# Values' projection as seven block products of halves, in one piece under the scores of head 0

## The chip, the cores and the metric

The kernel runs on one core of one Trainium2 chip. The metric is the device time of one execution in microseconds; before the change the median of three runs is 856.49 us (856.48 to 856.85). TensorE is called PE here, VectorE DVE, ScalarE ACT, GpSimd POOL, and SyncE, which issues most DMAs, SP. Each engine works through its own queue in order.

## What is computed

One block of a streaming encoder on 512 tokens of 1024 features, in float32. Cut to what matters here:

```python
xn = rmsnorm(x, norm_mix_g)
q, k, v, xr, gr, ga, gb = split(xn @ w_in)           # seven parts of 1024 columns each
ya = chunked_band_attention(q, k, v, rel_table) @ w_attn_out   # 16 heads of 64
yb = (rg_lru(conv(xr)) * gelu(gr)) @ w_rnn_out
h = x + (sigmoid(ga) * ya + sigmoid(gb) * yb) @ w_o
gu = rmsnorm(h) @ w_ffn_in
out = rmsnorm(h + (silu(g) * up) @ w_ffn_out)
```

The values `v = xn @ W_v` are a product of 512x1024 by 1024x1024. `W_v` is a slice of `w_in`.

## The kernel before

Every float32 operand is held as two parts, a high one (`hi`, a copy on ACT, line L82) and the remainder (`lo`, a subtraction on DVE, line L83); the helper `split` issues both. One product of two such operands is three matmuls, in the helper `mm3` (lines L76, L77, L78). `whl_...` is a weight tile in both parts, `raw_...` the same tile as it came from memory.

PE works through these stages: norms and transposes of x (until 38 us); the gated branch (`xr`, `gr`, `gb`, convolution and scan), until 166 us, with the first pair of heads' queries and keys `q0`, `k0` at its end; values' tiles of group 0; scores of head 0; `yb`, the product with `w_rnn_out` (189 to 233 us); the sixteen heads with the rest of `q`, `k`, `v` and gate `ga` between them (233 to 432 us); `ya`; the product with `w_o`; the FFN.

Values: `v_tile(gr, t)` computes 128 tokens by 512 columns, 24 matmuls with tokens stationary. There are two groups of columns of four tiles each; group 0 stands ahead of `yb`, group 1 between the heads.

Heads: PE's order is written by hand. In the loop over heads each head h is: transposes of its probabilities (`transposed`, tiles `pT`, split into `pp`), scores of head h+1 (`scores`, tiles `s`), the tiles named in `laid[h]` left of the bar, the product with the values (`weigh`, tile `o`, added up in `oacc`), the tiles right of the bar. After the scores DVE adds the bias and reduces (L740), ACT takes the exponential (L741), DVE the reciprocal of the sums `rl` (L742) and POOL scales the four blocks of probabilities `p` (L744), which the next transposes read.

`k_tile` leaves `kh` and `kl` of two heads: for each, ACT copies the own half of the partitions (L686), DVE subtracts (L687), ACT copies into the other half (L688) and POOL casts (L689). Scores of the pair's first head read both halves.

Products with `w_o` and the FFN matrices are already made as seven products of halves instead of eight. For these the sums of weight blocks are made early, by `spill` and `spill_in`: SP loads four blocks (tiles `spill...`), DVE forms the four sums one on the other, SP stores them to memory (`sums...`), and the stage that uses them loads them again. Here `w_o`'s are made in the gated branch, those of `w_ffn_out`'s first unit and of the FFN-in tiles `fg2`, `fu2` during `yb`.

Of the kernel before, what the change touches and what calls it, by code (L numbers as in the profile page):

```python
# [36 lines left out]
def block_kernel(ctx: ExitStack, tc: tile.TileContext, x, norm_mix_g, w_in, b_merge, rel_table,  # L37
# [478 lines left out]
    def rnn_gates(j, xc, xch, g):  # L516
# [22 lines left out]
        dve.scalar_tensor_tensor(ti[:], ti[:], 1.0, xc[:], ALU.add, ALU.mult)  # L539
        return j, u, a, ti, g  # L540

    def rnn_scan(j, u, a, ti, g):
        dve.scalar_tensor_tensor(ti[:], ti[:], 0.5, u, ALU.mult, ALU.mult)
        dve.tensor_tensor_scan(u, a[:], ti[:], 0.0, ALU.mult, ALU.add)
        dve.scalar_tensor_tensor(u, u, 0.5, g[:], ALU.mult, ALU.mult)
        if j % 2 == 0:
# [2 lines left out]
        act.activation(o[:, 0], u, AF.Copy)
        pool.tensor_sub(o[:, 1], u, f(o[:, 0]))  # L550
        return o
# [47 lines left out]
    def spill(w, unit, to, r):  # L599
# [4 lines left out]
        for out_, i, a_, b_ in ((b11, 0, b12, b11), (b12, 2, b22, b12), (b22, 1, b22, b11), (b21, 3, b21, b22)):  # L604
# [4 lines left out]
            if out_ is b22:  # L609
                sp.dma_start(out=to[0][:], in_=b11)  # L610

    def spill_of(w, u, pl, tag, bufs):
        name, unit, to = (("o", units_o, sums_o) if w is w_o else ("f", units, sums_d))
# [89 lines left out]
    for k in (4, 6):
        homes["v0", k] = (aw, "v", 8, 1)

    def v_tile(gr, t):
        wv = weights(f"v{gr}")
        po = mm_tile(f"po_v{gr}_{t}", "mm" if gr else "t")
        for k in range(KT):
            mm3(po[:], xnT[k][:, 0, t * P:(t + 1) * P], xnT[k][:, 1, t * P:(t + 1) * P],  # L710
                wv(0, k, every), wv(1, k, every), k == 0, k == KT - 1)
        v = aw.tile([P, 4, 4, HD], F32R, tag="v", bufs=8, name=f"v{gr}_{t}")
        split(v[:, :, 0::3], v[:, :, 1:3], po[:].rearrange("p (a b d) -> p a b d", a=4, b=2))
        vs.setdefault(gr, []).append(v)
# [49 lines left out]
    def weigh(h, pp):  # L764
        pr, e = divmod(h, 2)
        own, other = halves(e)
        if e == 0:
            oacc.append(tg_.tile([P, S], F32, tag="tg", name=f"oacc{pr}"))
        acc = oacc[pr]
        po = mm_tile(f"o{h}")  # L770
        for kb in range(NT):
            i, lo, n = ((0, 0, 512), (1, 0, 384), (2, 0, 256), (2, 256, 128))[kb]
            st = vs[pr // 4][kb][:, pr % 4, 2 * e:2 * e + 2].rearrange("p a d -> p (a d)")
            for part in range(2):
                pe.matmul(po[:, S - n:S], st, pp[i][:, part, lo:lo + n], start=kb == 0 and part == 0, stop=kb == NT - 1 and part == 1)  # L775
        act.activation(acc[own, :], po[other, :], AF.Copy)
# [21 lines left out]
    kinds = {"q": q_tile, "k": k_tile, "v": lambda t: v_tile(1, t), "g": gate_a}  # L798

    def project_all(names):  # L800
        for n in names.split():
# [590 lines left out]
```

## Time and profile before

| What | Value |
|---|---|
| Median of the runs | 856.49 us (856.48 to 856.85) |
| Profiled execution | span 854.7 us on the page; no device time of its own is listed |
| PE busy | 845.1 us (99%) |
| DVE, ACT, POOL busy | 642.1, 507.5, 107.5 us |
| Chain that ended last | PE 97% |
| DMA | 135.70 MB, mean 159 GB/s |

The span runs from the first instruction to the last. The chain follows back from the last instruction to what released each step; a share of 97% on PE says that nearly all of the span is PE going from one of its instructions to the next. In rows of groups, the two numbers after the bar are busy microseconds and mean nanoseconds of one instruction; behind the second bar is the idle time ahead of them on that engine. In a timeline row the first two numbers are start and duration in microseconds.

### The profile page before, as it was taken

To read this page: it belongs to the slowest core of one execution; us is meant where nothing else is said; L and a number is where in the kernel's file an instruction comes from. 1 tells how busy PE (TensorE), PEld (TensorE's weight loads), DVE (VectorE), ACT (ScalarE), POOL (GpSimd) and SP (SyncE) were. 2 spreads that over 40 slices of the span, in tenths; PEclk is the share of its full clock that TensorE was granted. 3 is DMA by queue.
4 is the path that set the end of the run, shared out by engine and by line. 5 is a ranking of instruction groups with operands and counts; after the bars stand their busy time and mean duration, and the time that the engine had idled before them with its cause. 6 is when DMAs were issued, how large, how long until landed. Compare 5 with 4: busy or idle time off the path is not lost.

```text
span 854.7 us, 13069 instructions
## 1 busy us (share of the span) xinstructions
PE 845.1 (99%) x4884; PEld 741.0 (87%) x4884; DVE 642.1 (75%) x972; ACT 507.5 (59%) x877; POOL 107.5 (13%) x152
## 2 busy tenths in 40 slices
PE   8999999999999999999999999999999999999997
PEld 6977887888888888888888889999999999988885
DVE  5789767635665657557668877988999887699985
ACT  7678687741366657666654546556555555385555
POOL 2324302200113313223200000000000001000002
PEclk9999999999999999999999999999999999999999
DMA  8594332429852113323156541665666343886622
GB/s 275 190 313 164 99 99 67 120 79 362 274 157 75 59 52 101 98 75 111 50 175 244 157 164 50 201 234 166 241 203 215 100 123 99 275 297 205 209 74 98
DMA packets 103663, 135.70 MB, mean 159 GB/s; under 512 B 6832, under 2 KB 77088, under 8 KB 103600
## 3 DMA queue, kind: packets, MB, share of 16 engines
q1 hardware_dynamic: 99920, 127.20, 45.4%
q10 hardware_dynamic: 3680, 7.67, 2.9%
q8 instruction: 38, 0.62, 0.3%
q14 instruction: 25, 0.20, 0.1%
HBM read 115.93 MB, written 18.92 MB: 158 GB/s over the span
## 4 chain that ended last, share of the span: by engine, by line
PE 97%; ACT 1%; DVE 1%; DMA 1%; issue 0%; POOL 0%; SPq 0%; ACTq 0%; DVEq 0%
PE po_out L76 4%; PE po_out L77 4%; PE po_out L78 4%; PE o L775 2%; PE p_fu L78 2%; PE p_fg L78 2%; PE p_fu L76 2%; PE p_fg L77 2%; PE p_fg L76 2%; PE p_fu L77 2%; PE pT L755 2%; PE po_gb L76 2%; PE po_gb L77 2%; PE po_ga L76 2%; PE po_v L76 2%; PE po_ga L78 2%
## 5 line engine op out<-in xcount | busy, mean ns | idle before, releaser
L744 POOL TENSOR_SCALAR p<-p,rl 128x128 f32<-128x128 f32 (+1 forms) x64 | 39.6, 637 | 164.6 <-DVE rl L742 164.5
L741 ACT ACTIVATE p<-p,m 128x128 f32<-128x128 f32 (+1 forms) x64 | 35.8, 562 | 13.8 <-DVE m L740 13.8
L1104 POOL TENSOR_TENSOR act_lo<-act,act_hi 128x1024 fp32r<-128x1024 f32 x1 | 2.4, 2414 | 294.3 <-ACT act_hi L1103 294.3
L83 DVE TENSOR_TENSOR pp<-pT,pp 128x384 fp32r<-128x384 f32 (+1 forms) x48 | 27.8, 596 | 9.8 <-ACT pp L82 9.7
L740 DVE CUSTOM_DVE_ANT_0 p<-s,bias 128x128 f32<-128x128 f32 (+1 forms) x64 | 29.2, 483 | 3.9 <-PE s L737 3.8
L83 DVE TENSOR_TENSOR whl_t<-raw_t,whl_t 128x1024 fp32r<-128x1024 f32 x26 | 31.9, 1226 | 0.3 <-ACT whl_t L82 0.3
L83 DVE TENSOR_TENSOR whl_qk<-raw_qk,whl_qk 128x1024 fp32r<-128x1024 f32 x16 | 21.6, 1348 | 11.3 <-ACT whl_qk L82 11.3
L76 PE MATMUL po_gr<-xnT,whl_gr 128*128 128x512 f32 (+1 forms) x80 | 28.2, 354 | 0.1
L82 ACT ACTIVATE whl_t<-raw_t 128x1024 fp32r<-128x1024 f32 x26 | 27.2, 1047 | 1.5 <-PE po_h L78 1.5
L77 PE MATMUL po_xr<-xnT,whl_xr 128*128 128x512 f32 (+1 forms) x80 | 27.8, 353 | 0.0
L77 PE MATMUL po_gr<-xnT,whl_gr 128*128 128x512 f32 (+1 forms) x80 | 27.6, 346 | 0.0
L78 PE MATMUL po_gr<-xnT,whl_gr 128*128 128x512 f32 (+1 forms) x80 | 27.6, 348 | 0.0
L78 PE MATMUL po_xr<-xnT,whl_xr 128*128 128x512 f32 (+1 forms) x80 | 27.3, 346 | 0.0
L76 PE MATMUL po_xr<-xnT,whl_xr 128*128 128x512 f32 (+1 forms) x80 | 26.7, 353 | 0.6 <-ACT xnT L362 0.6
L83 DVE TENSOR_TENSOR whl_fg_s<-s_fg,whl_fg_s 128x1024 fp32r<-128x1024 f32 x20 | 24.4, 1222 | 2.9 <-ACT whl_fg_s L82 2.9
L83 DVE TENSOR_TENSOR whl_fu_s<-s_fu,whl_fu_s 128x1024 fp32r<-128x1024 f32 x20 | 24.3, 1221 | 2.9 <-ACT whl_fu_s L82 2.8
L82 ACT ACTIVATE whl_qk<-raw_qk 128x1024 fp32r<-128x1024 f32 x16 | 16.8, 1052 | 16.0 <-PE po_yb L78 8.8
L76 PE MATMUL po_gb<-xnT,whl_gb 128*128 128x512 f32 x64 | 25.3, 395 | 0.2 <-DVE xc L501 0.2
L82 ACT ACTIVATE whl_fu_s<-s_fu 128x1024 fp32r<-128x1024 f32 x20 | 21.0, 1056 | 7.3 <-PE q_fu L78 2.6
L76 PE MATMUL po_ga<-xnT,whl_ga 128*128 128x512 f32 x64 | 25.3, 395 | 0.0
L77 PE MATMUL po_gb<-xnT,whl_gb 128*128 128x512 f32 x64 | 25.1, 393 | 0.0
L82 ACT ACTIVATE whl_fg_s<-s_fg 128x1024 fp32r<-128x1024 f32 x20 | 21.1, 1056 | 6.8 <-DVE s_fg L195 3.9
(421 smaller groups left out, 3261.8 us busy)
## 6 DMA issues: line engine op xcount, KB each, us to landing
raw_fg<-in_w_ffn_in_dram SPq DMA_DIRECT2D x22, 512.0 KB, 3.7
raw_fu<-in_w_ffn_in_dram SPq DMA_DIRECT2D x22, 512.0 KB, 5.0
raw_t<-sums SPq DMA_DIRECT2D x20, 512.0 KB, 4.5
raw_qk<-in_w_in_dram SPq DMA_DIRECT2D x32, 256.0 KB, 3.2
spillf<-in_w_ffn_out_dram SPq DMA_DIRECT2D x16, 512.0 KB, 8.0
sums<-spillf SPq DMA_DIRECT2D x16, 512.0 KB, 4.6
raw_b<-in_w_ffn_out_dram SPq DMA_DIRECT2D x15, 512.0 KB, 4.3
raw_xr<-in_w_in_dram SPq DMA_DIRECT2D x8, 512.0 KB, 4.9
```

What stands on the lines that cost most here:

```text
L76: pe.matmul(o, sh, mh, start=start, stop=False, skip_group_check=parts)
L77: pe.matmul(o, sh, ml, start=False, stop=False, skip_group_check=parts)
L78: pe.matmul(o, sl, mh, start=False, stop=stop, skip_group_check=parts)
L82: act.activation(hi, src, AF.Copy)
L83: dve.tensor_sub(lo, src, f(hi))
L740: dve.tensor_tensor_reduce(prob[qb][:], scs[qb], bias[:, S - w:S], -1.0, 3e38, ALU.add, ALU.min, nmax[:, qb:qb + 1])
L741: act.activation(prob[qb][:], prob[qb][:], AF.Exp, bias=nmax[:, qb:qb + 1], scale=-1.0, accum_out=lsum[:, qb:qb + 1])
L744: pool.tensor_scalar(prob[qb][:], prob[qb][:], rl[:, qb:qb + 1], 1.0, ALU.mult, ALU.mult)
L755: pe.transpose(pt[:, at * P:(at + 1) * P], prob[qb][:, kb * P:(kb + 1) * P], ident[:])
L775: pe.matmul(po[:, S - n:S], st, pp[i][:, part, lo:lo + n], start=kb == 0 and part == 0, stop=kb == NT - 1 and part == 1)
L1104: pool.tensor_sub(lo[:], o[:], f(hi[:]))
```

## The change

Values are computed as seven products of blocks. Features and weights are cut in halves both ways: tokens 0 to 255 and 256 to 511, inner dimension in halves, columns in halves. With blocks `a11` to `a22` of xn and `b11` to `b22` of `W_v`, sums `s1` to `s4` of the first and `t1` to `t4` of the second, the products are `a11 b11`, `a12 b21`, `s1 t1`, `s2 t2`, `s4 b22`, `s3 t3`, `a22 t4`. Each has 256 tokens (two tiles of 128) by 512 columns by 512 inner, that is 2 x 12 matmuls of 128x512. Sums that chain through several products stay in PSUM; others are copied out by ACT (`v_keep`) and added by DVE (`v_finish`).

The whole projection stands between `yb` and the heads, with scores of head 0 between the two token tiles of `s3 t3`. The sums of `W_v` are made in the gated branch, in the place of those of `w_o`; `w_o`'s are made around the start of `yb`; those of `w_ffn_out`'s first unit, `fg2` and `fu2` are called for in heads 1, 4 and 6. The sums of xn are made during `yb`. Group 1's tiles go from `laid`.

```diff
-    laid = ("q1 k1 | v0", "q2 |", "k2 | v1", "q3 |", "k3 | v2", "q4 v3 |", "k4 | q5", "k5 | g0",
-            "g1 |", "q6 | g2", "k6 | g3", "q7 |", "k7 | g4", "g5 |", "g6 |", "g7 |")
+    laid = ("q1 k1 |", "q2 |", "k2 |", "q3 |", "k3 |", "q4 |", "k4 |", "q5 | g0",
+            "k5 | g1", "q6 |", "k6 | g2", "q7 | g3", "k7 | g4", "g5 |", "g6 |", "g7 |")
...
-    for t in range(NT):
-        v_tile(0, t)
...
     for j in range(0, KT, 2):
         if j >= 4:
-            at_once(spill_of(w_o, j // 2 - 2, early, "spill", 4))
+            at_once(spill_of(w_v, j // 2 - 2, early, "spill", 4))
...
+    def wv_part(name, u):
+        n = sources[name]
+        raw = wp.tile([P, 2, S], F32, tag="raw", bufs=3, name=f"raw_v{name}_{u}")
+        sp.dma_start(out=raw[:], in_=sums_v[u][n][:] if name[0] == "t" else square(w_v, units_v[u][n[0]], n[1]))
+        hl = wp.tile([P, 2, 2, S], F32R, tag="whl", bufs=4, name=f"whl_v{name}_{u}")
+        split_pair(hl, raw[:])
+        wv[name, u] = hl
...
+    def v_multiply(a, b, banks, start, tokens=range(2)):
+        for i in tokens:
+            tok = slice(i * P, (i + 1) * P)
+            for u in range(2):
+                w = wv[b, u]
+                for k in range(2):
+                    mm3(banks[i][:], xv_at(a, u, k, 0, tok), xv_at(a, u, k, 1, tok), w[:, 0, k], w[:, 1, k],
+                        start and u == 0 and k == 0, u == 1 and k == 1, parts=True)
...
+    def v_split(gr, t, src):
+        v = v_of(gr, t)
+        split(v[:, :, 0::3], v[:, :, 1:3], by_heads(src))
+
+    def v_finish(gr, t, bank):
+        whole = kept[gr, t // 2][:, t % 2]
+        dve.tensor_add(whole, bank[:], whole)
+        v_split(gr, t, whole)
...
     for j in range(KT):
+        if j in (0, 2):
+            at_once(spill_of(w_o, j // 2, aw, "v", 8))
+        if j in (3, 4, 5, 6):
+            xv_sum(("s1", "s2", "s4", "s3")[j - 3])
         if j == 6:
-            prob = scores(0)
-        if j == 0:
-            at_once(spill_of(w_ffn_out, 0, aw, "v", 8))
-        if j in (2, 4):
-            spill_in(("fg2", "fu2")[j // 2 - 1], aw, "v", 8)
+            blocks_v("b11")
...
+        v_multiply("s3", "t3", chain, False, (0,))
+        v_finish(1, 2, chain[0])
+        prob = scores(0)
+        v_multiply("s3", "t3", chain, False, (1,))
+        v_finish(1, 3, chain[1])
+        weights("qk1", 0)
+        for i in range(2):
+            v_multiply("a22", "t4", chain, False, (i,))
+            v_split(0, 2 + i, chain[i][:])
...
+    def spill_at(h):
+        if h in (1, 4, 6):
+            r = [big(n, [P, 2, 4, 256] if h > 1 else [P, 2, 2, S], F32, f"spill_a{h}_{n}") for n in ((2, 3) if h == 1 else (2 + h // 6,))]
+            if h == 1:
+                at_once(spill(w_ffn_out, units[0], sums_d[0], [r[n // 2][:, n % 2] for n in range(4)]))
+            else:
+                spill_in(("fg2", "fu2")[h // 6], r[0])
...
         for h in range(HEADS):
+            spill_at(h)
             pp = transposed(h, prob)
```

Line numbers of the changed program are other ones than those of the profile: `kh`'s copies are L687 and L689 there, reductions L727, the exponential L728, `rl` L729.

On PE the tile of values behind `k1` goes, and head 1's transposes follow the product `o0`. ACT's queue from the end of `k1` on, before; `kh1` is the high part of the keys of heads 2 and 3, first copied for its own half, then for the other:

```order
L686 ACTIVATE kh1_2245<-po_k1_2220 64x512
L82 ACTIVATE whl_qk3_0_2367<-raw_qk3_0_2364 128x1024
L776 ACTIVATE oacc0_2255<-o0_2256 64x512
L688 ACTIVATE kh1_2245<-po_k1_2220 64x512
L686 ACTIVATE kh1_2245<-po_k1_2220 64x512
L688 ACTIVATE kh1_2245<-po_k1_2220 64x512
L82 ACTIVATE v1_0_2304<-po_v1_0_2279 128x4x2x64
L82 ACTIVATE pp1_0_2307<-pT1_0_2310 128x512
L82 ACTIVATE pp1_1_2308<-pT1_1_2317 128x384
```

And now:

```order
L687 ACTIVATE kh1_2417<-po_k1_2392 64x512
L82 ACTIVATE whl_qk3_4_2519<-raw_qk3_4_2516 128x1024
L763 ACTIVATE oacc0_2427<-o0_2428 64x512
L82 ACTIVATE pp1_0_2453<-pT1_0_2456 128x512
L82 ACTIVATE pp1_1_2454<-pT1_1_2463 128x384
L689 ACTIVATE kh1_2417<-po_k1_2392 64x512
L687 ACTIVATE kh1_2417<-po_k1_2392 64x512
L82 ACTIVATE pp1_2_2455<-pT1_2_2469 128x384
L689 ACTIVATE kh1_2417<-po_k1_2392 64x512
```

The copies of `pp1_0` and `pp1_1` now stand ahead of `kh1`'s copy for the other half. Behind `k2`, `k3` and `k4` the order of ACT's rows up to that copy is as before.

DVE's queue from the last reduction of head 0 (`p0_3`, with its accumulator `m0`) to what follows the reciprocal `rl0`, before:

```order
L740 ISA p0_3_2023,m0_2018<-s0_2_2026,bias0_2011 128x512
L740 ISA m0_2018 128x1
L83 TENSOR_TENSOR whl_qk1_4_2058<-raw_qk1_4_2055,whl_qk1_4_2058 128x1024
L742 RECIPROCAL rl0_2019<-l0_2017 128x4
L816 SCALAR_TENSOR_TENSOR zb6_441<-zb6_441,po_yb6_2048 128x512
L83 TENSOR_TENSOR whl_v1_0_2173<-raw_v1_0_2171,whl_v1_0_2173 128x1024
```

And now (`spill_a1` are the blocks of `w_ffn_out`, `kept` and `v` belong to values):

```order
L727 ISA p0_3_2208,m0_2203<-s0_2_2211,bias0_2196 128x512
L727 ISA m0_2203 128x1
L603 TENSOR_TENSOR spill_a1_2_2439<-spill_a1_2_2439 128x1024
L83 TENSOR_TENSOR v1_2_2193<-kept1_2_2085,v1_2_2193 128x4x128
L871 TENSOR_TENSOR kept1_2_2085<-pv_mm1_1968,kept1_2_2085 128x512
L83 TENSOR_TENSOR whl_qk1_0_2252<-raw_qk1_0_2249,whl_qk1_0_2252 128x1024
L729 RECIPROCAL rl0_2204<-l0_2202 128x4
L83 TENSOR_TENSOR whl_qk1_4_2258<-raw_qk1_4_2255,whl_qk1_4_2258 128x1024
L83 TENSOR_TENSOR v1_3_2246<-kept1_2_2085,v1_3_2246 128x4x128
```

Three instructions more stand between the last reduction and the reciprocal, the first of which reads blocks that SP loads after the fifth product. In the same way two subtractions for `fu2` come ahead of `rl2`, and one for `fg2` ahead of DVE's part of `q1` and `k1`.

More of the change, by code (lines that the diff above doesn't have):

```diff
@@ L390, in block_kernel @@
     act.copy(gm[:], gm_p[:, 0:8])
-    _, xnT = features(xnp, "xn", "xnT")
+    xnT_all, xnT = features(xnp, "xn", "xnT")
     def xn_at(k, part, half):
@@ L540, in rnn_gates, with big @@
         return j, u, a, ti, g
+    def big(n, shape, dtype, name):
+        return rnp.tile(shape, dtype, tag=f"big{n}", bufs=1, name=name)
     def rnn_scan(j, u, a, ti, g):
@@ L546, in rnn_scan @@
         if j % 2 == 0:
-            rnn_pairs.append(rnp.tile([P, 2, 2, S], F32R, tag="big", bufs=4, name=f"rnn{j}"))
+            rnn_pairs.append(big(j // 2, [P, 2, 2, S], F32R, f"rnn{j}"))
         o = rnn_pairs[-1][:, j % 2]
@@ L610, in spill @@
                 sp.dma_start(out=to[0][:], in_=b11)
+    w_v = w_in[:, C_V:C_V + D]
+    units_v = (0, 2), (1, 3)
+    sums_v = [drams(f"sums_v{u}") for u in range(2)]
     def spill_of(w, u, pl, tag, bufs):
[L613 removed]
+        name, unit, to = {id(w_v): ("v", units_v, sums_v), id(w_o): ("o", units_o, sums_o)}.get(id(w), ("f", units, sums_d))
         r = [pl.tile([P, 2, S], F32, tag=tag, bufs=bufs, name=f"spill{name}{u}_{n}")[:] for n in range(4)]
@@ L617, in block_kernel, with spill_in @@
     first_sums = {f"f{w}2": [dr.tile([P, 2, 4, P], F32, name=f"sums_f{w}2_{n}") for n in range(2)] for w in "gu"}
-    def spill_in(name, pl, tag, bufs):
+    def spill_in(name, both):
         col = chunks[index[name]][1][0][1]
-        r = [pl.tile([P, 4, CW], F32, tag=tag, bufs=bufs, name=f"spill{name}_{n}") for n in range(2)]
+        r = [both[:, n] for n in range(2)]
         for n in range(2):
-            sp.dma_start(out=r[n][:], in_=w_ffn_in[n * S:(n + 1) * S, col:col + CW].rearrange("(k p) e -> p k e", p=P))
+            sp.dma_start(out=r[n], in_=w_ffn_in[n * S:(n + 1) * S, col:col + CW].rearrange("(k p) e -> p k e", p=P))
         s2, s3, s4, s1 = (r[n][:, :, i * P:(i + 1) * P] for n in range(2) for i in range(2))
@@ L701, in block_kernel @@
     vs = {}
[L703 to L714, printed above, removed]
     biases = []
@@ new lines, in blocks_v, with xn_block, xv_sum @@
+    def blocks_v(name):
+        for u in range(2):
+            wv_part(name, u)
+    def xn_block(which, part):
+        i, j = int(which[0]) - 1, int(which[1]) - 1
+        return f(xnT_all[:, 4 * j:4 * j + 4, part, (lo_half, hi_half)[i]])
+    def xv_sum(name):
+        o = xv32[name] = aw.tile([P, 4, 256], F32, tag="v", bufs=8, name=f"xv32_{name}")
+        o = o[:]
+        add, sub = "tensor_add", "tensor_sub"
+        if name in ("s1", "s3"):
+            (first_, a_), (then, b_) = (("add", "21"), ("add", "22")) if name == "s1" else (("add", "11"), ("sub", "21"))
+            getattr(pool, add if then == "add" else sub)(o, xn_block(a_, 1), xn_block(b_, 1))
+            dve.tensor_add(o, o, xn_block(a_, 0))
+            getattr(dve, add if then == "add" else sub)(o, o, xn_block(b_, 0))
+        elif name == "s2":
+            dve.tensor_sub(o, xv32["s1"][:], xn_block("11", 0))
+            dve.tensor_sub(o, o, xn_block("11", 1))
+        else:
+            dve.tensor_sub(o, xn_block("12", 0), xv32["s2"][:])
+            dve.tensor_add(o, o, xn_block("12", 1))
@@ new lines, in by_heads, with v_of, v_keep @@
+    def by_heads(ap):
+        return ap.rearrange("p (a b d) -> p a b d", a=4, b=2)
+    def v_of(gr, t):
+        v = aw.tile([P, 4, 4, HD], F32R, tag="v", bufs=8, name=f"v{gr}_{t}")
+        vs.setdefault(gr, {})[t] = v
+        return v
+    kept = {}
+    def v_keep(gr, t, bank):
+        at = gr, t // 2
+        if at not in kept:
+            kept[at] = aw.tile([P, 2, S], F32, tag="qk", bufs=3, name=f"kept{gr}_{t}")
+        act.activation(kept[at][:, t % 2], bank[:], AF.Copy)
+    def v_split(gr, t, src):
+        v = v_of(gr, t)
+        split(v[:, :, 0::3], v[:, :, 1:3], by_heads(src))
@@ L814, in block_kernel @@
         po = mm_tile(f"po_yb{j}")
-        project(po, weights(f"yb{j - j % 2}"), j % 2, rnn)
+        project(po, weights(f"yb{j - j % 2}", 1 if j < 6 else 0), j % 2, rnn)
         dve.scalar_tensor_tensor(zB[j], zB[j], 1.0, po[:], ALU.add, ALU.mult)
     with tc.manual_schedule(engines={mybir.EngineType.PE}):
+        chain, second = ([mm_tile(f"pv_{tag}{i}", tag) for i in range(2)] for tag in ("mm", "t"))
+        fifth = [ss.tile([P, S], F32, tag="s", bufs=2, name=f"pv_s{i}") for i in range(2)]
@@ new lines, in block_kernel @@
+        for n, name in enumerate(("s1", "s2", "s4", "s3")):
+            if n < 2:
+                xv_split(n, name)
+        v_multiply("a11", "b11", chain, True)
+        for i in range(2):
+            v_keep(0, i, chain[i])
+        blocks_v("t1")
+        v_multiply("a12", "b21", second, True)
+        for i in range(2):
+            v_finish(0, i, second[i])
+        blocks_v("t2")
+        xv_split(2, "s4")
+        v_multiply("s1", "t1", fifth, True)
+        for i in range(2):
+            v_keep(1, 2 + i, fifth[i])
@@ new lines, in block_kernel @@
+        blocks_v("b22")
+        xv_split(3, "s3")
+        v_multiply("s2", "t2", chain, False)
+        for i in range(2):
+            v_keep(1, i, chain[i])
+        blocks_v("t3")
+        v_multiply("s4", "b22", fifth, False)
+        for i in range(2):
+            v_finish(1, i, fifth[i])
+        blocks_v("t4")
+        v_multiply("s3", "t3", chain, False, (0,))
[3 more added lines that the diff above has]
+        v_finish(1, 3, chain[1])
@@ L818, in block_kernel @@
+    with tc.manual_schedule(engines={mybir.EngineType.PE}):
         for h in range(HEADS):
+            spill_at(h)
             pp = transposed(h, prob)
```

31 lines of the change are left out of this document (20 added, 11 removed).

## The prediction

> **What bounds the kernel now.** I read the page's totals first, then the chain that ended last, then PE's waits, then busy time by stretch.
>
> ```profile
> span 854.7 us, 13069 instructions
> PE 845.1 (99%) x4884; PEld 741.0 (87%) x4884; DVE 642.1 (75%) x972; ACT 507.5 (59%) x877; POOL 107.5 (13%) x152
> PE 97%; ACT 1%; DVE 1%; DMA 1%; issue 0%; POOL 0%; SPq 0%; ACTq 0%; DVEq 0%
> PE busy L312 <- DVE eps_t L318: 1.2, 1, 1.2
> PE pt_mix L358 <- DVE xs_mix L351: 1.1, 1, 1.1
> PE po_xr L76 <- ACT xnT L362: 0.6, 2, 0.4
> PE po_gb L76 <- DVE xc L501: 0.2, 1, 0.2
> ```
>
> The first two lines give the totals, the third the chain; the last four are all of PE's waits, 3.1 us in the whole program. In the table of stretches the columns after the window are the sum of PE, then PE, PEld, DVE, ACT and POOL busy with counts, the granted clock, the DMA share and GB/s.
>
> ```profile
> 50.00:166.00 116.00, 116.00 (x521) 92.33 (x520) 87.72 (x104) 86.27 (x115) 30.79 (x24) 1.00 0.44 139
> 166.00:189.00 23.00, 23.00 (x106) 19.15 (x105) 9.96 (x16) 11.36 (x19) 1.56 (x3) 1.00 0.18 52
> 189.00:233.00 44.00, 44.00 (x196) 36.44 (x195) 27.66 (x34) 12.11 (x14) 2.21 (x5) 1.00 0.95 316
> 233.00:432.00 199.00, 199.00 (x1035) 171.04 (x1034) 123.03 (x263) 126.49 (x270) 48.56 (x87) 1.00 0.30 87
> ```
>
> From 50 us on PE is never idle, at full granted clock. So every PE instruction that goes is worth its issue time, every new wait of PE costs its length, and what the other engines gain or lose counts only as such a wait. The stretches are the gated branch, values' first group, `yb`, and the heads.
>
> **What is removed.** Values' projection takes 8 tiles of 24 matmuls.
>
> ```profile
> 166.58 0.39 PE L76 MATMUL po_v<-whl_v,xnT 128*128 128x512 f32 x1
> 177.23 0.39 PE L78 MATMUL po_v<-whl_v,xnT 128*128 128x512 f32 x1
> 177.46 0.22 PE L736 MATMUL s<-kh,q 128*128 128x128 f32 x1
> ```
>
> These are the first and last of 48 matmuls of two tiles and what follows: (177.46 - 166.58)/48 = 0.2267 us each; the 0.39 is a pipelined duration. Seven products of halves are 7 x 2 x 12 = 168 matmuls of the same shape instead of 192: 24 x 0.2267 = **5.44 us less**. [...]
>
> **Work beside the products.** They need 14 loads and splits of weights instead of 8, sums of features, copies and adds. Prices from the groups (busy, mean ns):
>
> ```profile
> L83 DVE TENSOR_TENSOR whl_v<-raw_v,whl_v 128x1024 fp32r<-128x1024 f32 x8 | 9.7, 1220 | 2.4 <-ACT whl_v L82 2.2
> L82 ACT ACTIVATE whl_v<-raw_v 128x1024 fp32r<-128x1024 f32 x8 | 8.4, 1057 | 5.2 <-PE po_yb L78 4.8 <-DMA raw_v<-in_w_in_dram 0.3
> L83 DVE TENSOR_TENSOR v<-po_v,v x8: 684/692/692, 175.3 to 316.2; 128x512 fp32r<-128x512 f32 x8
> raw_v<-in_w_in_dram SPq DMA_DIRECT2D x8, 512.0 KB, 5.1
> spillf<-in_w_ffn_out_dram SPq DMA_DIRECT2D x16, 512.0 KB, 8.0
> raw_fg<-in_w_ffn_in_dram SPq DMA_DIRECT2D x22, 512.0 KB, 3.7
> ```
>
> DVE in the 38 us of the products: 14 weight splits and 2 feature splits at 1.22, 6 adds and 8 value splits at 0.69, 29 us; ACT about 25. A product that finishes two tiles has 2 x 1.22 + 4 x 0.69 = 5.2 of DVE against 5.44 of PE. Loads are 14 x 0.52 MB in 38 us, 193 GB/s, against 316 carried in `yb`. I cost this at nothing: PE covers it, with a product in reserve between splitting and use. If loads take 8.0 instead of 5.1, the tightest product waits up to 3. In `yb` DVE drops 4 subtractions at 1.22 and 8 at 0.69 and gets 8 sums of features and some subtractions for `w_o`, within the 16 us it idles there; POOL gets two 128x1024 sums. Nothing.
>
> **`w_o`'s sums ahead of `yb`.** Values' spill takes the place of `w_o`'s in the early stage, like for like: nothing. But `w_o`'s own loads are now issued behind `qk0` around 147, and three subtractions enter DVE's queue among the last scans, ahead of what POOL needs.
>
> ```profile
> 163.01 3.33 POOL L550 TENSOR_TENSOR rnn<-u,rnn 128x512 fp32r<-128x512 f32 x2 [7.92 <-ACT rnn L549]
> ```
>
> `rnn6` and `rnn7` are ready at 166.34; before, `yb` read them after 189. Now `yb` starts at 166.6 and reads its pairs 6 and 7 about 4.1 us later. Three subtractions at 1.22 move the 166.3 to some 170, a slack of 1 us. Six 0.52 MB loads at 316 GB/s land by 158, when the subtractions come up. Zero, at most 3 if the loads are late.
>
> **Heads without a filler after k.** Before, a tile of values followed each `k`. Now `k2`, `k3`, `k4` are followed by the head's product, the next transposes, and then the scores that read that `k`.
>
> ```profile
> 270.05 1.37 PE L775 MATMUL o<-pp,v 128*128 128x512 f32 x8
> 270.25 0.59 ACT L686 ACTIVATE kh<-po_k 64x512 fp32r<-64x512 f32 x1 [1.20 <-PE po_k L78]
> 270.74 1.05 ACT L82 ACTIVATE whl_qk<-raw_qk 128x1024 fp32r<-128x1024 f32 x1
> 271.81 0.60 ACT L776 ACTIVATE oacc<-o 64x512 f32<-64x512 f32 x1
> 272.44 0.59 ACT L688 ACTIVATE kh<-po_k 64x512 fp32r<-64x512 f32 x1
> 260.98 1.37 PE L775 MATMUL o<-pp,v 128*128 128x512 f32 x8
> 263.22 0.31 PE L736 MATMUL s<-kh,q 128*128 128x128 f32 x1
> ```
>
> ACT finishes the second copy of `kh` 2.98 us after `o` starts (273.03 - 270.05), in the same queue order as in the changed program, and PE reaches scores 2.24 after `o` starts (263.22 - 260.98). So PE waits 0.74 at each: 3 x 0.74 = **2.2 us more**. Bounds: 0, if ACT has no weights to split there (1.05 less), and 0.74 + 1.05 each if it has one more, 5.4.
>
> For `k1`, ACT has `pp1_0` and `pp1_1` ahead of that copy.
>
> ```profile
> 253.86 1.36 ACT L82 ACTIVATE pp<-pT 128x512 fp32r<-128x512 f32 x3
> ```
>
> Three take 1.36, two some 0.9: 2.98 + 0.9 - 2.24 = **1.6 us more**; at least 0.7 (without them). DVE's `kl1` there stands behind a subtraction for `fg2`, whose loads wait for the store of `w_ffn_out`'s sum and land only just in time; late by 3 makes it 4.
>
> **The softmax of head 0.** Scores of head 0 end 8.2 us ahead of its transposes (the second half of the sixth product and the seventh: 36 matmuls).
>
> ```profile
> 255.47 0.23 PE s L737
> 259.07 0.18 DVE L742 RECIPROCAL rl<-l 128x4 f32<-128x4 f32 x1 [1.22 <-ACT p L741]
> 259.45 2.05 POOL L744 TENSOR_SCALAR p<-p,rl 128x128 f32<-128x128 f32 x4 [7.69 <-DVE rl L742]
> 268.60 3.02 POOL L744 TENSOR_SCALAR p<-p,rl 128x128 f32<-128x128 f32 x4 [6.88 <-DVE rl L742]
> 269.09 1.41 DVE L83 TENSOR_TENSOR whl_qk<-raw_qk,whl_qk 128x1024 fp32r<-128x1024 f32 x1 [0.68 <-ACT whl_qk L82]
> ```
>
> Normally scaling ends 5.8 after the scores (255.70 to 261.50). Now DVE does four things between the last reduction and `rl0`: a subtraction for `w_ffn_out`, a split and an add of values, and a weight split, 1.22 + 0.69 + 0.69 + 1.22. Reductions end some 1.9 after the scores; the subtraction's loads are issued when the fifth product ends, 4 us ahead of the scores' end, and at 5.1 to 8.0 land 1.1 to 4.0 behind it, two in a row, so about 2.9. Then 2.9 + 3.8 + 0.2 puts `rl0` at 6.9, and scaling, 2.05 to 3.02, ends at 9.0 to 9.9; PE needs the last block 8.4 after. That is 0.6 to 1.5, and I take **0.9 us more**; bounds 0 (loads at 3.7) and 3 (both loads late).
>
> The two POOL rows bear on why: with a split of weights running, the four scalings took 3.02 instead of 2.05. [...]
>
> `rl2` stands behind two subtractions for `fu2`, 2 x 0.69; its scaling then ends at about the time PE comes: **0.2**, up to 4 if their loads, issued behind four stores, are late. The remaining splits and stores in the heads (DVE has 76 us idle there) cost nothing; FFN stages keep their order.
>
> **Sum.** -5.44 + 2.2 + 1.6 + 0.9 + 0.2 = -0.5 us. The profiled execution spans 854.7; the median of the runs is 856.49, so some 1.8 lie around the span. Span 854.2, time **856.0**. About 0.2% (1.7 us) is what a measurement of this kernel can tell from no change.
>
> **Rivals.**
> 1. *Saving kept.* ACT and DVE reach the copies and reciprocals in time, because gaps elsewhere let them run ahead. For it: ACT is busy 126 of 199 us in the heads. Against: the copy's 2.98 is a chain from `po_k`'s end, not load. With no wait 851.05; with half of them 853.5.
> 2. *Late loads at the reciprocals and `kl1`* (slower). The FFN subtractions stand in DVE's in-order queue ahead of `rl0`, `kl1` and `rl2`, and each waits for loads that wait for stores. It decides once loads land past the 5.1 I assumed; at the 8.0 of `spillf` each of three places gives up to 2.9 more: 3 x 2.9 - 0.5 = +8, 864; with one or two of them 858.5 to 861. For it: `spillf` is the slowest row. Against: that median is from a stretch with a DMA share of 0.95, the heads have 0.30.
> 3. *The saving is not there.* PE's count falls, but `yb` begins against unfinished `rnn` and products wait for weights, 3 us each at most: about 859 with the waits of the heads.
>
> **How the numbers follow.** My sum holds with 0.42 (853.5 to 858.5), rival 1 with 0.31, rival 2 with 0.20, rival 3 with 0.07. Of the first, 0.32 lies within 0.2% and 0.05 on either side; rival 1 is faster, rivals 2 and 3 slower. So faster 0.36, same 0.32, slower 0.32. The range reaches from the full saving, 851.2, to 861.0, which leaves out the far half of rival 2.
>
> **What the profile after would show.** PE with 24 fewer matmuls and 839.7 us of busy work, `pv` 168 strong; PE waits at scores on ACT `kh`, one of 1.6 and three of 0.7; a wait of about 0.9 at the first transposes on POOL `p`; none inside the products and none at `po_yb`. I am wrong if these waits are missing (rival 1), if DVE idles on DMA ahead of `rl` (rival 2), or if PE waits inside `pv` or `yb` (rival 3).

## The result, and the profile after

The changed kernel takes 864.73 us (median; 862.95 to 869.55) against 856.67 us of the kernel before (856.48 to 857.90) on the same chip: a ratio of 1.0101, interval 1.0083 to 1.0119. It is 8.1 us slower, where 856.0 was forecast with a range to 861.0. The profiled execution took 865.66 us, near the median.

The page of the changed kernel, totals and chain:

```profile
span 863.9 us, 13113 instructions
PE 845.4 (98%) x4860; PEld 738.8 (86%) x4860; DVE 680.2 (79%) x1004; ACT 520.9 (60%) x893; POOL 123.9 (14%) x154
PE 86%; DVE 4%; DMA 4%; ACT 3%; issue 2%; POOL 1%; SPq 0%; ACTq 0%; DVEq 0%; POOLq 0%
```

The 24 matmuls are gone from the count (4884 to 4860), yet PE's busy time is what it was: matmuls took longer behind a wait (0.50 us at 174.16, where `yb` waits, instead of 0.39) and at a lower clock (0.63, below). The chain that ended last was 97% PE; now 14% of it runs over other engines and transfers. PE's waits (total, times, longest) show the first of the new ones:

```profile
PE s L723 <- ACT kh L689: 4.7, 3, 3.8
PE po_yb L77 <- POOL rnn L549: 2.2, 2, 1.2
PE s L724 <- POOL kl L690: 1.6, 2, 1.1
...
PE pT L742 <- POOL p L731: 0.6, 2, 0.3
```

The table of stretches places them; columns as in the prediction's table (sum of PE, busy PE, PEld, DVE, ACT, POOL, clock, DMA share, GB/s):

```profile
166.00:210.00 44.00, 41.81 (x184) 33.97 (x183) 38.85 (x36) 13.35 (x16) 16.48 (x6) 1.00 0.60 200
210.00:250.00 40.00, 40.00 (x181) 33.24 (x180) 31.08 (x40) 26.86 (x39) 0.33 (x2) 1.00 0.64 198
250.00:300.00 50.00, 43.98 (x216) 36.90 (x215) 39.68 (x80) 30.39 (x65) 15.98 (x23) 0.93 0.78 242
```

The first row is `yb`: PE idles 2.2 us. The second is the products: no idle time at all. The third is heads 0 to 3 and the scores of head 4: PE idles 6 us and its granted clock averages 0.93. The same by stage, worked out from the starts of the first matmuls of each stage in PE's timeline (the stages up to `qk0` end at 166.6 and 166.5):

| Stage, us | before | after | difference |
|---|---|---|---|
| values' group 0, or the seven products, with scores of head 0 | 22.6 | 39.4 | +16.8 |
| `yb` | 44.0 | 46.3 | +2.3 |
| heads, up to `ya` (before: with group 1, 96 x 0.2267 = 21.8) | 198.6 | 188.4 | -10.2 |
| `ya` to the end | 422.9 | 423.2 | +0.3 |

Without group 1 the heads were 198.6 - 21.8 = 176.8; they are 11.6 longer now. One thing stands in different rows: before, the last two matmuls of head 0's scores, 0.45 us, fall into `yb`. Counted alike, `yb` goes from 43.5 to 46.3 (+2.8), and the products take 39.4 - 22.6 - 0.45 - 21.8 = -5.4 us. The two profiled spans differ by 863.9 - 854.7 = 9.2 us (the medians by 8.1): -5.4 saved, +11.6 in the heads, +2.8 in `yb`, +0.3 behind.

The one long wait is at the scores of head 2. The chain there, in order of time (start, length, what):

```profile
255.04 5.05 DMA sums<-spill_a
...
260.58 6.90 DMA spill_a<-in_w_ffn_in_dram
...
268.28 1.22 DVE whl_qk L83
...
270.98 0.69 DVE kl L688
...
271.72 2.15 POOL kl L690
...
273.92 0.48 PE s L724
```

And DVE's timeline at the subtraction (in brackets the idle time before it, and what ended it):

```profile
267.67 0.69 DVE L627 TENSOR_TENSOR spill_a<-spill_a 128x512 f32<-128x512 f32 x1 [3.54 <-DMA spill_a<-in_w_ffn_in_dram]
```

A store of `w_ffn_out`'s sums frees the buffer of `fg2`'s blocks at 260.1; their load takes 6.9 us; DVE, whose first subtraction for `fg2` waits 3.54 us for it, reaches `kl1` that much late; POOL's cast of `kl1` takes 2.15. Waits are also sized by spacing: how much later PE's matmuls start behind one another than the same pair of tiles does in the kernel before. That puts this wait at 5.5 us (268.2 to 273.9). What follows shows in windows of 3.41 us:

```profile
268.99:272.40 3.41, 0.07 (x1) 0.07 (x1) 3.32 (x6) 1.07 (x4) 0.68 (x1) 1.00 0.84 252
272.40:275.81 3.41, 2.28 (x8) 2.00 (x9) 3.38 (x6) 0.99 (x2) 1.46 (x1) 0.50 0.84 212
275.81:279.23 3.42, 3.42 (x10) 2.65 (x9) 2.77 (x10) 2.61 (x8) 0.61 (x1) 0.50 1.07 335
```

PE's timeline in the last of them:

```profile
277.07 0.63 PE L78 MATMUL po_q<-xnT,whl_qk 128*128 128x512 f32 x1
277.50 0.63 PE L76 MATMUL po_q<-xnT,whl_qk 128*128 128x512 f32 x1
```

After a window with PE idle the granted clock is 0.50 for 6.83 us, and matmuls of 512 columns start 0.43 us apart instead of 0.227: another 2.5 us by spacing. `yb` waits for its last pair of `rnn`, for which two rows answer, of DVE and of POOL:

```profile
157.03 1.61 DVE L603 TENSOR_TENSOR spillo<-spillo,spillo 128x1024 f32<-128x1024 f32 x1 [3.18 <-DMA spillo<-in_w_o_dram]
...
168.78 5.33 POOL L549 TENSOR_TENSOR rnn<-u,rnn 128x512 fp32r<-128x512 f32 x2 [10.60 <-ACT rnn L548]
```

DVE idles 3.2 us on `w_o`'s load with the scans queued behind it, and POOL's subtractions take 5.33 instead of 3.33 us.

### The profile page after: what moved, and what is told of

Same layout as the page of the kernel before. It is cut to its first block, busy times and chain, and to the rows that moved or that the text cites. A ratio compares the mean times of both kernels' runs of the same rounds, so it can differ in the third digit from the quotient of the medians.

```text
span 863.9 us, 13113 instructions
## 1 busy us (share of the span) xinstructions
PE 845.4 (98%) x4860; PEld 738.8 (86%) x4860; DVE 680.2 (79%) x1004; ACT 520.9 (60%) x893; POOL 123.9 (14%) x154
## 4 chain that ended last, share of the span: by engine, by line
PE 86%; DVE 4%; DMA 4%; ACT 3%; issue 2%; POOL 1%; SPq 0%; ACTq 0%; DVEq 0%; POOLq 0%
PE po_out L76 4%; PE po_out L77 4%; PE po_out L78 4%; PE p_fu L76 2%; PE p_fu L78 2%; PE p_fg L78 2%; PE p_fg L77 2%; PE p_fg L76 2%; PE p_fu L77 2%; PE o L762 2%; PE po_ga L76 2%; PE po_ga L78 2%; PE po_ga L77 2%; PE po_ya L76 2%; PE po_ya L78 2%; PE po_ya L77 2%
## 5 line engine op out<-in xcount | busy, mean ns | idle before, releaser
L731 POOL TENSOR_SCALAR p<-p,rl 128x128 f32<-128x128 f32 (+1 forms) x64 | 41.6, 669 | 105.5 <-DVE rl L729 105.4
L728 ACT ACTIVATE p<-p,m 128x128 f32<-128x128 f32 (+1 forms) x64 | 35.8, 563 | 11.3 <-DVE m L727 11.3
L727 DVE CUSTOM_DVE_ANT_0 p<-s,bias 128x128 f32<-128x128 f32 (+1 forms) x64 | 29.0, 483 | 1.9 <-PE s L724 1.7
L77 PE MATMUL po_yb<-rnn,whl_yb 128*128 128x512 f32 x64 | 25.1, 393 | 2.2 <-POOL rnn L549 2.2
L723 PE MATMUL s<-kh,q 128*128 128x128 f32 (+1 forms) x64 | 21.3, 354 | 4.7 <-ACT kh L689 4.7
L76 PE MATMUL po_q<-xnT,whl_qk 128*128 128x512 f32 x64 | 25.7, 402 | 0.0
L76 PE MATMUL po_gb<-xnT,whl_gb 128*128 128x512 f32 x64 | 25.3, 395 | 0.2 <-DVE xc L497 0.2
L78 PE MATMUL po_q<-xnT,whl_qk 128*128 128x512 f32 x64 | 25.4, 397 | 0.0
```

Source lines behind the costliest of these rows:

```text
L76: pe.matmul(o, sh, mh, start=start, stop=False, skip_group_check=parts)
L77: pe.matmul(o, sh, ml, start=False, stop=False, skip_group_check=parts)
L78: pe.matmul(o, sl, mh, start=False, stop=stop, skip_group_check=parts)
L723: pe.matmul(scs[qb], qs, kh[:, e, 0:w], start=True, stop=False)
L727: dve.tensor_tensor_reduce(prob[qb][:], scs[qb], bias[:, S - w:S], -1.0, 3e38, ALU.add, ALU.min, nmax[:, qb:qb + 1])
L728: act.activation(prob[qb][:], prob[qb][:], AF.Exp, bias=nmax[:, qb:qb + 1], scale=-1.0, accum_out=lsum[:, qb:qb + 1])
```

## Experiments

**The theory**: moved subtractions stand in DVE's queue ahead of what PE needs and wait there for late loads. **The first rival**: the heads lost the tiles of values that stood beside their chains, and copies of `kh` and the softmax are late whatever DVE does. **The second**: halves cost PE more than the count says; the products' stretch above already speaks against it. Runs are numbered e1 to e12, since the expectations refer to one another. The work that PE has between a head's scores and its transposes, while the softmax runs on the other engines, is called the softmax's cover.

**Loads held back (e1, e2).** A tiny ACT write into the buffers of `fg2` and `fu2`, which reads the scaled probabilities, lets their loads start only in heads 6 and 8.

```diff
-        if h in (1, 4, 6):
+        if h in (1, 6, 8):
+            for t in r:                                  # fg2 and fu2 alone
+                for n in range(2):
+                    act.activation(t[:, n, 0, 0:1], prob[3][:, 0:1], AF.Copy)
```

> The changed kernel, with the loads for the sums of fg2 and fu2 held back until the probabilities of heads 6 and 8 are ready, so that none of their subtractions stands in DVE's queue in heads 1 and 2. Theory A (the 5.5 us wait at the scores of head 2 comes from the subtraction for fg2 that waits for its loads, and PE's clock falls to half for 6.8 us because of that wait): the wait shrinks to 0.7 to 1.6 us, the clock stays at full, the 0.6 us wait at the transposes of head 2 goes; 864.7 - 3.9 to 4.8 - 2.7 - 0.6 = about 857. Theory B (the wait is ACT's queue, in which the copy of kh stands behind two pp copies and a weight split): the wait stays above 4 us and the time within 1 us of 864.7.

Measured: 864.58 us, ratio 1.0094 (1.008 to 1.0108). PE's waits:

```profile
PE pT L742 <- POOL p L731: 3.8, 6, 2.1
PE s L723 <- ACT kh L689: 2.0, 4, 0.6
```

And two stretches of the heads:

```profile
250.00:300.00 50.00, 48.19 (x255) 40.67 (x254) 38.63 (x83) 35.11 (x79) 16.16 (x28) 1.00 0.49 157
300.00:350.00 50.00, 45.69 (x220) 38.27 (x219) 32.94 (x72) 29.43 (x67) 15.75 (x24) 0.90 0.46 141
```

At the scores of head 2 the 3.8 us wait and the half clock are gone with the loads and subtractions that stood there. But the same subtractions now make the transposes of head 7 wait, with some 10 us of half clock behind it, worked out from the mean of 0.90 over the 50 us. DVE waits only 0.3 us for a load there; what is long is POOL's scaling of that head, 5.73 us beside three FFN subtractions and two splits of weights; in heads 0 to 9 of the kernel before four scalings take 2.05 to 3.02:

```profile
322.50 5.73 POOL L731 TENSOR_SCALAR p<-p,rl 128x128 f32<-128x128 f32 x4 [7.37 <-DVE rl L729]
```

The wait moved with the subtractions. With all three sets held so, in heads 4, 6 and 8:

> As e1, and the sums of w_ffn_out's first unit are held back too, until head 4. Theory A: besides what e1 gains, the wait at the first transposes (0.5 us) and DVE's wait of 2.1 us for these loads go: 0.5 us below e1, about 856.5. Theory B: as the changed kernel, 864.7. A third outcome: the held-back subtractions now stand ahead of the reciprocals of heads 5 and 7, and PE waits there; then the time lies above e1.

Measured: 871.48 us, 1.0181 (1.0159 to 1.0202), PE waiting in the two places where the subtractions now stand:

```profile
PE pT L742 <- POOL p L731: 7.4, 5, 4.0
```

The scalings ahead of these transposes, of heads 5 and 7, take 6.59 and 5.50 us on POOL. So a later place alone doesn't help: what counts is beside which work on POOL and PE the subtractions come to run.

**`yb` (e3).** The same tiny write, from the last `rnn`, holds `w_o`'s loads until `rnn7` is written.

```diff
+        if w is w_o:
+            for t in r:
+                act.activation(t[:, 0, 0:1], f(rnn_pairs[-1][:, 1, 1, 0:1]), AF.Copy)
```

> The changed kernel, with the loads of w_o for its sums held back until the last rnn pair is written, so that no subtraction for w_o stands among DVE's last scans. Theory A (the two waits in yb, 2.5 us together, come from DVE's wait of 3.2 us for w_o's loads and from its subtractions ahead of the last u): both waits go, 864.7 - 2.5 = 862.2. Rival: the loads only move into yb, where they delay yb's weights or the sums of xn, and new waits of the same size appear there; 864 to 866.

Measured: 863.58 us, 1.0083 (1.0069 to 1.0098). The stretch of `yb` and the heads' beginning:

```profile
166.00:210.00 44.00, 44.00 (x196) 36.44 (x195) 38.34 (x35) 15.71 (x25) 9.99 (x5) 1.00 0.76 274
250.00:300.00 50.00, 43.35 (x210) 36.41 (x210) 38.18 (x78) 29.49 (x66) 13.92 (x22) 0.93 0.74 228
```

`yb` no longer waits (43.5 us instead of 46.3), so the loads and subtractions for `w_o` ahead of the scans made that wait. The total gives back less than that: the wait at head 2 stays and is slightly longer, and head 0's transposes lose 1.3 us by spacing instead of 0.5.

**The clock (e4).** 24 matmuls whose result nobody reads stand between the transposes of head 1 and the scores of head 2 (`pe.matmul(unused[:], xnT[0][:, 0, 0:P], xnT[0][:, 0, :], ...)`), to keep PE busy through the wait.

> The changed kernel with 24 added matmuls of 128x512 whose result nobody reads (5.4 us of PE work at full clock), put between the transposes of head 1 and the scores of head 2, where PE waits 5.5 us. Theory A (PE's idleness there is what lowers its clock): the clock stays at full through heads 1 and 2 and the time falls by the 2.7 us that the low clock cost, to about 862. Rival (the low clock has another cause, or follows in any case): the clock still falls, and the time stays at 864.7 or rises.

Measured: 868.97 us, 1.0147 (1.0133 to 1.0161); the profiled execution took 866.37. The longest of PE's waits, and the stretch of the held wait:

```profile
PE pT L742 <- POOL p L731: 3.1, 4, 2.2
```
```profile
250.00:300.00 50.00, 46.27 (x237) 38.93 (x236) 38.32 (x76) 29.59 (x63) 14.71 (x23) 1.00 0.79 244
```

In this execution the clock stays at 1.00, where the changed kernel's averages 0.93 in the same stretch, so idling lowered it there; but the matmuls take the 5.4 us that the wait took, and the transposes of head 2 now wait, 2.2 us at the longest, for a softmax with two subtractions ahead of `rl2`. No time is won. The profiled execution is the fastest of the five; the other four show a mean clock of 0.994 or 0.995, as low as the changed kernel's 0.994, and where they lost it is not known.

**Subtractions held, not loads (e5).** Loads start early; ACT adds a zero, made from the scaled probabilities of that head, to a column that the first subtraction of a set reads, so that each set is held to heads 3, 7 and 9.

```diff
+    def hold_back(at, late):
+        act.activation(zero[:], late, AF.Copy, scale=0.0)
+        act.activation(at, at, AF.Identity, bias=zero[:])
...
-        if h in (1, 4, 6):
+        if h in (3, 7, 9):
```

> The changed kernel, in which the loads for the FFN sums go out as early as before, but the first subtraction of each of the three sets is held back until the probabilities of heads 3, 7 and 9 are ready, so that each finds its data long landed. Theory A2 (what costs is a subtraction at the head of DVE's queue that waits for its load, wherever it stands, and e1 and e2 only moved that): no wait of DVE on these loads, no low clock; what remains is 2.5 us in yb and about 0.5 at the scores behind each of k1 to k4; 856.6 - 5.4 + 2.5 + 2.0 + 0.3 = 856.0. Rival (the extra subtractions by themselves overfill DVE in the heads, late loads or not): a wait of over 1 us at transposes or scores stays, and the time stays above 860.

Measured: 862.85 us (860.06 to 864.85), 1.0065 (1.0049 to 1.0082); the profiled execution is the fastest, 860.06. In it no subtraction waits for a load any more and the wait at head 2 is gone; what PE waits for is left mostly at the transposes of head 4:

```profile
PE pT L750 <- POOL p L739: 2.4, 4, 1.3
PE s L731 <- ACT kh L697: 1.5, 3, 0.5
```

**Order of the copies of `kh` (e6).** In the changed kernel, ACT's copy into the other half is written ahead of DVE's `kl` (the two lines change places).

> The changed kernel, with ACT's copy of kh into the other half of the partitions written ahead of DVE's subtraction for kl instead of behind it, so that it need not wait for DVE. Theory A2: the waits of 0.5 us or so at the scores behind k2, k3 and k4 go (1.4 to 2.0 us together), while the long wait behind k1, which hangs on kl, stays: 864.7 - 1.7 = 863.0. Rival (the copy is late because ACT is busy with weight splits, not because of DVE): the waits stay, 864.7.

Measured: 866.67 us, 1.012 (1.0107 to 1.0133). PE's longest wait:

```profile
PE s L724 <- POOL kl L690: 6.5, 4, 5.6
```

ACT's copies are on time now, and PE waits as long for POOL's cast of `kl`: two chains end together, and shortening one alone gains nothing. The prediction's 0.74 had named ACT alone.

**Two of these together (e7, e8).** Subtractions held, and `w_o`'s loads held:

> e5 and e3 together: the subtractions for the FFN held back, and w_o's loads issued once the last rnn pair is written. If the gains add, yb's 2.5 us go from e5: 853.5, which is below the kernel before (856.6). If the later w_o loads delay what follows (weights of yb, sums of xn, values' first weights), the time is e5's or above.

Measured: 860.04 us (858.32 to 861.07), 1.0033 (1.0021 to 1.0046). With the order of `kh` besides (e8):

> e7 with the order of kh's copies of e6. If all the waits that I name are gone, what is left is the saving of 24 matmuls: 856.6 - 5.4 = 851.2, with 0.3 to 0.8 on top for the transposes of head 0, so 851.2 to 852.0. If it lies above 853, a part of the loss is still unnamed.

Measured: 861.08 us, 1.0053 (1.004 to 1.0066). What still holds up the transposes of head 4, in the first of these two kernels (start, duration; DVE, POOL, PE):

```profile
292.14 1.22 DVE L610 TENSOR_TENSOR spill_a<-spill_a,spill_a 128x1024 f32<-128x1024 f32 x1
293.28 0.17 DVE L740 RECIPROCAL rl<-l 128x4 f32<-128x4 f32 x1
293.39 1.23 DVE L610 TENSOR_TENSOR spill_a<-spill_a,spill_a 128x1024 f32<-128x1024 f32 x1
...
293.64 3.87 POOL L742 TENSOR_SCALAR p<-p,rl 128x128 f32<-128x128 f32 x4 [5.17 <-DVE rl L740]
...
297.56 0.66 PE L753 MATMUL pT<-ident,p 128*128 128x128 f32 x4 [1.30 <-POOL p L742]
```

No load is late here. One subtraction ahead of `rl4` and one beside POOL's scaling (3.87 us instead of 2.05) are enough for 3.1 us by spacing: head 4's softmax has a single tile as cover.

**The sums left out (e9, e10).** To tell the theory from the first rival, the loads and subtractions for the three FFN sets are left out and only the stores stay, of other data; in the second kernel those for `w_o` too.

> The changed kernel with the loads and subtractions for w_ffn_out, fg2 and fu2 left out; only the stores stay, of other data. Theory, the change costs what it costs because the moved subtractions wait for their loads in DVE's queue and PE's clock falls behind that wait: scores of head 2 lose 5.5 us of wait and 2.6 us of half clock, the transposes of heads 0 and 2 lose 0.5 each; the waits of 0.6 at the scores behind k2 to k4 and 2.5 at yb stay. -5.44 + 1.9 + 2.5 = -1.0, so 855.7 against 856.7 before. Rival, the heads wait without their fillers whatever DVE has to do: 860 or more, with PE waits over 5 us in the heads. Second rival, a product of halves costs PE as much as the tiles it replaces: 861, without waits.

> As the run before, and the loads and subtractions for w_o are left out too. Theory: the 2.5 us of yb go as well, -5.44 + 1.9 = -3.5, so 853.2; PE's only waits are the three of 0.6 behind k2 to k4. Rivals as for that run: 858 or more with waits in the heads, or 858.5 without waits.

Measured: 856.84 us, 1.0006 (0.9998 to 1.0015), and 858.97 us, 1.0031 (1.0019 to 1.0044). The waits of the first, and two of the second:

```profile
PE s L723 <- ACT kh L689: 1.8, 4, 0.5
PE po_yb L77 <- POOL rnn L549: 1.2, 1, 1.2
```
```profile
PE po_yb L76 <- ACT rnn L548: 2.1, 1, 2.1
PE s L723 <- ACT kh L689: 1.8, 4, 0.5
```

The FFN loads and subtractions together cost 864.73 - 856.84 = 7.9 us, nearly all of the loss; without them the heads take 180.3 us in both kernels instead of 188.4, at full clock. That is 1.1 us above the 855.7 expected: each of the four waits at scores costs 0.8 us by spacing, 3.2 together. The first rival (860 or more) falls, as a cause of more than these four waits; the second (861 without waits) falls too. The second kernel missed its 853.2: `yb` takes 49.6 us, part of it because the clock is at 0.50 for 6.83 us behind the wait of 2.1. With `w_o`'s subtractions gone, the sums of features moved up into their place ahead of the scans. The timeline there, POOL and DVE:

```profile
148.71 3.37 POOL L820 TENSOR_TENSOR xv_s<-xnT 128x1024 f32<-128x1024 f32 x1
...
149.74 2.88 DVE L534 SCALAR_TENSOR_TENSOR u<-u 128x512 f32<-128x512 f32 x1
```

A scan's operand takes 2.88 us (0.68 in the changed kernel) beside POOL's sum. So not the loads of `w_o` alone can make `yb` wait, but other work that stands ahead of the last scans too.

**Where a subtraction may stand (e11, e12).** Two versions with all sums made and `w_o`'s held. In one the subtractions are spread, one or two in each of heads 2 to 11; in the other they stay in three sets, called for in heads 7, 9 and 11 (`if h in (7, 9, 11)`), where the softmax has more cover.

> All sums are made, w_o's held until the last rnn is written, those of w_ffn_out one subtraction in each of heads 2 to 5, fg2's two in each of heads 6 and 7, fu2's one in each of heads 8 to 11, each held until that head's probabilities are scaled. Theory that crowding of subtractions between the reductions and the reciprocal makes the waits: no wait over 1 us at the transposes, no half clock, -5.44 + 1.9 + at most 0.3 in each of ten heads, 853 to 856.5. Rival, any two-source DVE work beside POOL's scaling delays the transposes: waits of 0.7 to 1 in most of heads 2 to 8, 858 to 860, as with the subtractions held in three heads (860.0).

> All sums are made, w_o's held until the last rnn is written; those of w_ffn_out are called for in head 7, fg2's in head 9 and fu2's in head 11, each set held until that head's probabilities are scaled. Heads 7, 8 and 11 have two tiles of 5.4 us beside the softmax. Theory, a subtraction costs PE nothing where the softmax has two tiles as cover: as with the FFN sums left out (856.8), and without yb's 1.6, 855.2; PE waits 0.6 at the scores behind k2 to k4, and at most 1 at the transposes of head 10, whose softmax has one tile. Rival, subtractions cost PE wherever they stand beside POOL's scaling: transposes of heads 8 to 12 wait 2 to 4 us, half clock behind them, 859 to 862.

Measured for the spread: 865.66 us, 1.0098 (1.0081 to 1.0116), far outside either expectation. PE's waits, and a stretch of the heads:

```profile
PE pT L752 <- POOL p L741: 6.0, 8, 1.9
```
```profile
300.00:350.00 50.00, 45.93 (x214) 38.35 (x213) 33.43 (x75) 31.63 (x79) 14.12 (x24) 0.90 0.52 153
```

Three heads with a single tile as cover (3, 5 and 7 by the times of the waits) each lost 2 to 3.5 us and then the clock (a mean of 0.97 from 250 to 300, and the row's 0.90). A subtraction is not the whole cause. In heads 3 and 7 the scaling starts 1.6 and 1.7 us after its reciprocal instead of 0.4, with a write to a `bias` tile ahead of it in POOL's queue; in head 3 that write waits for the load of `bias`:

```profile
283.85 0.15 POOL L435 MEMSET bias<- 64x64 f32 x1 [9.35 <-DMA bias<-ext_d]
```

So this run doesn't tell what spreading by itself costs. Measured for heads 7, 9 and 11: **856.26 us** (854.99 to 858.07) against 857.74 of the kernel before in the same runs, 0.9983 (0.9974 to 0.9992). It is the only version here that beats both kernels: by 0.17% against the kernel before, with an interval that stays below one, though within the 0.2% that the prediction took as the least that a measurement can tell. All of PE's waits from `yb` to `ya`, and the counterpart of head 4's rows above:

```profile
PE s L734 <- ACT kh L700: 2.0, 4, 0.6
```
```profile
331.52 1.23 DVE L610 TENSOR_TENSOR spill_a<-spill_a,spill_a 128x1024 f32<-128x1024 f32 x1
...
331.77 3.88 POOL L742 TENSOR_SCALAR p<-p,rl 128x128 f32<-128x128 f32 x4 [5.17 <-DVE rl L740]
...
337.94 1.26 PE L753 MATMUL pT<-ident,p 128*128 128x128 f32 x10
```

POOL's scaling is stretched to the same 3.88 us by the same subtraction, and ends at 335.65; PE, with a gate tile behind the queries, comes at 337.94 and doesn't wait. The same work in the same order cost a wait of 3 us in head 4 and nothing in head 8, which has two tiles. One tile can be enough too: `fg2`'s four subtractions (349.4 to 354.5) precede the softmax of head 10, which has a single tile; its reciprocal comes only at 358.9, with none of them in between, and PE doesn't wait there.

## Why the prediction was wrong

- **The saving of 5.44: right.** The products run without idle time (row 210 to 250) and take 39.4 us with scores of head 0 in every kernel here: 168 x 0.2267, and 1.3 for the scores. That the last version's median is 1.5 us below the kernel before, as -5.44 and +3.9 in its heads (180.7 instead of 176.8) would give, is partly luck: its profiled span, 854.3, is only 0.4 below the 854.7 of the kernel before. There `yb` starts 1.1 us later than before, and PE waits 1.1 us for POOL's `xch` in the gated branch.
- **The scores behind `k2`, `k3`, `k4`, 3 x 0.74: right in size.** In the runs without other waits the scores start 1.82 us behind the transposes instead of 1.03: 0.8 each. In the changed kernel it is 0.8 twice and 1.4 behind `k2`. The cause was half told: ACT's copy and POOL's cast end together.
- **`k1`'s scores, 1.6 (4 if late): the step that failed.** This place cost 8.0 us, 5.5 of wait and 2.5 of clock, twice even the 4. "Land only just in time" was named and then priced at nothing: I took 5.1 us for a load, and this one took 6.9 behind a store of 5.05, so that DVE stood 3.54 us. And the cast behind `kl1`, 0.61 us alone, took 2.15 beside DVE. Without the FFN subtractions the wait is 0.8; but there ACT copies `kh1` ahead of `pp1`, in the order of the other three, so the 1.6 for the changed order was not tested by itself.
- **The clock: a term that the sum lacked.** A wait cost its length in the sum; this one cost 2.5 us more, since half clock followed.
- **`yb` and `rnn`, "zero, at most 3": mis-sized.** Counted alike it measured 2.8, inside the bound, and the sum took zero. I had bounded DVE's three subtractions but neither DVE's wait for the first (3.2 us) nor POOL's 5.33 beside the rest.
- **Head 0's softmax, 0.9, and `rl2`, 0.2**: 0.5 by spacing at head 0's transposes; none at those of head 2, which follow the product `o1` at once. The wait on `p` that two expectations put at head 2 stands at head 3's transposes, behind `k2`, where no FFN subtraction runs.
- **Together:** 8.0 at `k1`, 1.4 + 0.8 + 0.8 behind the others and 0.5 at head 0 make 11.5, the heads' 11.6 but for rounding.
- **Rival 2**, late loads in DVE's in-order queue, had the mechanism and the sign, and got 0.20. That its price, 864, came out is luck: it put 2.9 us at each of three places, and one place lost 8.0, a part of it by the clock. Its reason against, that the heads' DMA share was 0.30 on the whole, was read from the kernel before; the stores and loads that the change itself puts there, beside the weights, raised it to 0.78 (250 to 300).

Two things are open. The changed kernel spreads by 6.6 us between executions where the kernel before spreads by 1.4; slower executions mostly show a lower mean clock (0.990 at 869.55 and 0.994 at 865.66, 0.997 and 0.995 at 863.80 and 862.95), but only the profiled ones show which wait halved it. And whether the load of 6.9 us was slow by the traffic around it, by its place behind the store or by both was not tried apart.

## What to carry to other kernels

Work that is moved "where the engine has time" must be placed by what is queued behind it: an in-order engine that waits for a load holds up all that follows (DVE stood 3.54 us for `fg2`'s blocks, and the scores of head 2 came 5.5 us late), and a subtraction between a reduction and its reciprocal, or beside the scaling behind it, costs PE unless the work beside that softmax is longer than the chain (3.1 us by spacing in head 4 with one tile, nothing in head 8 with two). Count the cover in tiles at the very place: two tiles hid what one did not. Putting the extra work together where there is cover won; the one version that spread it lost, but not by the spreading alone. Price a wait of PE by its length and by the clock that may be lost behind it: here 5.5 us of wait cost 2.5 more, a wait of 2.1 had 6.83 us of half clock behind it, and one of 3.1 by spacing had half clock behind it in one run and none in another.

## What the runs showed of the hardware

**Half clock came in multiples of 3.41 us.** The stretches of clock 0.50 behind waits are 6.83 us long in the changed kernel (272.39 to 279.22) and in the one without sums (173.26 to 180.09), twice 3.41. In the run with all three sets of loads held (e2) the mean clocks, 0.96 from 166 to 210 and 0.83 from 300 to 350, make some 3.5 and 17 us of half clock, about one and five times 3.41. In the changed kernel the clock is at 0.50 at the end of the program too, from 859.48 on, and that is 587.09 us behind 272.39, 172 times 3.413. PE did not always idle throughout the 3.41 us ahead of half clock. Two such windows, in the kernel with both holds and in the one without sums:

```profile
295.46:298.87 3.41, 1.87 (x14) 1.49 (x15) 3.19 (x4) 1.44 (x4) 2.19 (x3) 1.00 0.68 248
```
```profile
169.85:173.26 3.41, 1.29 (x6) 0.74 (x5) 3.35 (x5) 1.07 (x2) 0.39 (x1) 1.00 0.00 0
```

PE was busy 1.87 and 1.29 us of them, and the clock of the next 3.41 us is 0.51 and 0.50. The first belongs to the wait at head 4's transposes. With the subtractions alone held (e5) the same wait, 3.1 us by spacing in both, lay over the two windows below, and the clock stayed at 1.00 in them and, with a mean of 0.999 over the whole execution, behind them:

```profile
293.06:296.47 3.41, 2.51 (x13) 1.75 (x11) 3.35 (x5) 2.08 (x5) 2.54 (x4) 1.00 0.79 258
296.47:299.88 3.41, 2.11 (x16) 1.99 (x16) 3.19 (x5) 1.67 (x4) 1.47 (x2) 1.00 0.60 185
```

So the same wait was followed by half clock in one run and not in the other. What decides it no run shows, nor do the rows give a bound for the idle time: in the run with `w_o`'s loads held, a window with 1.70 us busy (264.74 to 268.15) left the clock of the next at 1.00.

**POOL and DVE took longer beside each other.** Beside DVE's subtractions with two inputs, POOL's cast took 2.15 instead of 0.61 us, four scalings 3.87 and 5.73 instead of 2.05, two `rnn` 5.33 instead of 3.33; beside a POOL sum of 3.37 us it was DVE that took 2.88 instead of 0.68, and it ended 0.54 us after POOL did (152.62 against 152.08). What one of them lost was not the other's whole length: 2.20 us for DVE beside that sum, and 0.97 for the four scalings of the prediction's rows (3.02 instead of 2.05) beside a split of 1.41. By what the two hold each other up, no run shows.
